# A ScalarE function set with logarithm and exponential together, loaded by hand at four places of a one-core diffusion layer

## The chip, the cores and the metric

The kernel runs on one core of one Trainium2 chip. The metric is the device time of one execution in microseconds (us), as a median over runs. Inside the core the trace has these engines: PE (TensorE matmul, with PEld for its weight loads), DVE (VectorE), ACT (ScalarE), POOL (GpSimd) and SP (SyncE, which issues most DMA transfers). Each engine takes its instructions in the order in which they were written to its queue; engines wait for each other through semaphores.

[...]

## The reference

One layer with 1024 latent tokens and 256 context tokens, width 1024. Cut to the parts in which a logarithm or an exponential stands:

```python
def rms_norm(x, w):
    y = xf * lax.rsqrt(jnp.mean(xf * xf, axis=-1, keepdims=True) + EPS)

px = modulate(rms_norm(x, norm1_w[i]), sh1, sc1) @ w_in[i]      # and the same for the context
dn_x, _, _ = gated_deltanet(px[..., :DN_IN], ...)               # conv + SiLU, decay exp(..), chunked scan
qx, kx, vx = na_qkv(px[..., DN_IN:], q_norm_w, k_norm_w)        # rms_norm per head of q and k
na_x = neighborhood_attention(qx, kx, vx, kc, vc, rpb, rows)    # softmax
x = x + g1 * (concat([dn_x, na_x]) @ w_out[i])
x = x + g2 * swiglu(modulate(rms_norm(x, norm2_w[i]), sh2, sc2), w_ffn_in[i], w_ffn_out[i])
...
```

## The kernel before

Everything is held with channels on the 128 partitions and tokens along the free dimension. Matmuls are in single precision, mostly as three products of a high and a low part, so each weight block is cut into `whi`/`wlo` (or `uhi`/`ulo`) by a CAST on ACT and a subtraction on DVE or POOL.

The program runs through these stages, in order of time:

- **Start.** Sums of squares, then the first norm: `rs` by a logarithm (L779) and an exponential (L781, times -0.5) on ACT, then the modulated tokens `hh`/`hl` (L752, L753, L759) and the first two blocks of the input projection.
- **Input projection.** A list of jobs: convolution blocks `k`, `q`, `v`, gates `z`, attention blocks `nk` and `nq`, and two wide jobs with tokens as rows. While PE multiplies job n, the job before it is finished. For `k`, `q`, `v` and `z` that takes the function SiLU (L529, L483). For `nk` and `nq` it is a norm by head: PE sums the squares `cr` into a PSUM bank `m` or `pr`, ACT takes the logarithm (L549) and then the exponential (L551 for `nq`, L553 for `nk`), DVE multiplies the block `cacc` by the result (L561), ACT rounds it to 16 bits (`hl`, L566 or L573), DVE forms the rest (L567, L574). Meanwhile two background generators run: the decay tables and block inverses (`decay_tables`, L836 to L888, exponentials; the inverse's copies `N`, L944, and its DVE chain L952/L954), and then `preps`, which build the triangular factors of each chunk: an exponential on `e` (L1022), `fx` copies (L1018), products in the PSUM banks `pr`, their copies `kk` on ACT (L1035) and `y` on DVE (L1043).
- **Scan and attention.** Two scans (forward and backward) run beside the neighbourhood attention; softmax is an exponential on ACT (L365), after a maximum on DVE (L363) and before a scaling on DVE (L367); PE then transposes (L106). The scan's copies on ACT are `u` (L1271) and `s` (L1283).
- **Output projection and second norm.** `normed(0)` and `normed(1)`: PE sums the squares `acc` (DVE, L1498), ACT takes logarithm and exponential (L1506, L1507) into `rs`, DVE scales the tokens `x` by it (L1614), ACT adds the shift and casts (L1618, L1619), DVE forms the low part (L1622).
- **FFN.** Products over saved sums of quadrants (L1638 forms a sum, L1608/L1609 cut it), SiLU (L1707, L1757), DVE additions out of PSUM (L1756, L1759), modulation work on weights `wad` that arrive by DMA (L253, L255), weights cut by L1464, L1468, L1469. From here to the end PE is fed from these streams.

The order on each queue is set by a scheduling layer that looks at the program with costs of its own; a few instructions are pinned to the written order by `tc.keep_in_program_order`. PSUM tiles are named by tag, with a number of buffers: in the input projection `blk` has 4, `m` and `pr` have 2 each. So a product into `pr` must wait until the product two before it was copied out.

Of the kernel before, what the change touches and what calls it, by code (L numbers as in the profile page):

```python
# [9 lines left out]
F32 = mybir.dt.float32  # L10
F32R = mybir.dt.float32r
F16 = mybir.dt.float16
I32 = mybir.dt.int32
AF = mybir.ActivationFunctionType
OP = mybir.AluOpType
# [76 lines left out]
def hybrid(ctx, tc, a, dbg):  # L92
    nc = tc.nc
    act, dve, pool, sp = nc.scalar, nc.vector, nc.gpsimd, nc.sync
# [12 lines left out]
            return tc.keep_in_program_order(i) if self.pinned else i  # L107

    pe = Tensor()

    def pools(stack, name, side=None, bufs=1, **kw):
        if side:
            kw["side"] = side
        return stack.enter_context(tc.tile_pool(name=name, bufs=bufs, reuse_waits="tile", **kw))
# [50 lines left out]
    nv_d = dram.tile([T, 512], F32, name="nv_d", tag="nv_d")  # L165
    nq_d = dram.tile([NAH, 2, ND, L], F16, name="nq_d", tag="nq_d")
    nk_d = dram.tile([2, NAH, ND, T], F16, name="nk_d", tag="nk_d")
    vw_d = dram.tile([4, 512, 512], F32, name="vw_d", tag="vw_d")
# [28 lines left out]
    def rsqrt(r, x, y):  # L197

        dve.tensor_scalar(y.bitcast(I32), x.bitcast(I32), 1, None, op0=OP.logical_shift_right)
        dve.tensor_scalar(r.bitcast(I32), y.bitcast(I32), -1.0, float(0x5F3759DF), op0=OP.mult, op1=OP.add)  # L200
        for _ in range(3):
# [97 lines left out]
    def attention(nw):  # L299

        def load(hd):
            qs = nw.tile([128, L], F16, name="qs", tag="qs", bufs=4)
            kh = nw.tile([128, T], F16, name="kh", tag="kh", bufs=4)
            kl = nw.tile([128, T], F16, name="kl", tag="kl", bufs=4)
            sp.dma_start(qs, nq_d[hd].rearrange("i d t -> (i d) t"))
            for i in range(2):
                sp.dma_start(kh[i * 64:i * 64 + 64], nk_d[0, hd])
                sp.dma_start(kl[i * 64:i * 64 + 64], nk_d[1, hd])
            return qs, kh, kl
# [111 lines left out]
    with ExitStack() as bs:  # L421
# [8 lines left out]
        def bank(name="m"):  # L430

            if len(psum) == 1:
                return psum[0].tile([128, 512], F32, name=name, tag="ps")
            return psum[1].tile([128, 512], F32, name=name, tag=name, bufs=4 if name == "blk" else 2)
# [19 lines left out]
        class Block:  # L454
# [22 lines left out]
            def evac(self):  # L477
                t0, kind, i = self.t0, self.kind, self.i
                if kind == "z":
                    zt = (zo[0].tile([128, T], F32, name="zt", tag="zt") if zo else  # L480
                          cp.tile([128, T], F32, name="zt", tag="kx", bufs=3))
                    for p, s0, n in self.pss:
                        act.activation(zt[:, s0:s0 + n], p[:, :n], AF.Silu)  # L483
                    sp.dma_start(zT_d[:, i], zt[:, t0:])
                    return
                self.acc = acc = cp.tile([128, T], F32, name="cacc", tag="cacc", bufs=2)
                conv = kind in "qkv"
                blk = {"q": 0, "k": 4, "v": 8}.get(kind, 0) + i
                if not conv or len(psum) == 1:
                    for p, s0, n in self.pss:  # L490
                        act.activation(acc[:, s0:s0 + n], p[:, :n], AF.Copy, scale=cw[:, blk, 2:3] if conv else 1.0)
                if not conv:
                    return
                if len(psum) == 1:
                    for p, s0, n in self.pss:
                        lo, hi = (0, CT) if s0 < CT else (CT, T)
                        for tap in (0, 1, 3, 4):
                            o = tap - 2
                            d0, d1 = max(lo, s0 - o), min(hi, s0 + n - o)
                            dve.scalar_tensor_tensor(acc[:, d0:d1], p[:, d0 + o - s0:d1 + o - s0],  # L500
                                                     cw[:, blk, tap:tap + 1], acc[:, d0:d1],
                                                     op0=OP.mult, op1=OP.add)
                    return
                raw = cp.tile([128, T], F32, name="cr", tag="cr", bufs=2)
                for p, s0, n in self.pss:
                    act.copy(raw[:, s0:s0 + n], p[:, :n])
                self.later = self.taps(raw, acc, blk)
# [18 lines left out]
            def silu(self):  # L526
                acc, t0 = self.acc, self.t0
                if self.kind in "qkv":
                    act.activation(acc[:, t0:], acc[:, t0:], AF.Silu)  # L529
                if self.kind in ("q", "nq", "nk"):  # L530
                    self.r = cp.tile([128, T], F32, name="cr", tag="cr", bufs=2)
                    act.activation(self.r[:, t0:], acc[:, t0:], AF.Square)

            def norm(self):

                kind, acc, t0, i = self.kind, self.acc, self.t0, self.i
                if kind in "vz":
                    return int
                if kind == "k":
                    sp.dma_start(kT_d[:, i], acc)  # L540
                    return int
                r = self.r
                if kind == "q":
                    sp.dma_start(qT_d[:, i], acc[:, t0:])
                    return int
                for s0, n in self.segs:
                    p = bank("pr" if kind == "nk" and s0 >= 768 else "m")
                    pe.matmul(p[:, :n], M[C_BD2], r[:, s0:s0 + n], start=True, stop=True)
                    act.activation(r[:, s0:s0 + n], p[:, :n], AF.Ln, bias=b_eps, scale=1.0 / ND)  # L549
                if kind == "nq":  # L550
                    act.activation(r[:, t0:], r[:, t0:], AF.Exp, scale=-0.5, bias=b_naq)  # L551
                else:
                    act.activation(r[:, t0:], r[:, t0:], AF.Exp, scale=-0.5)  # L553
                return self.split

            def split(self):
# [5 lines left out]
                                         op0=OP.mult, op1=OP.mult)  # L562
                hl16 = cp.tile([128, 2, T], F16, name="hl16", tag="kx", bufs=3)
                h16, l16 = hl16[:, 0], hl16[:, 1]
# [115 lines left out]
        with ExitStack() as xs:  # L680
# [52 lines left out]
            def sums(ps, k):  # L733

                for k in (k, k + 1):
                    sq = xp.tile([128, T], F32, name="sq", tag="sq", bufs=4)
                    act.activation(sq, xt[k], AF.Square)
                    if k % 2 == 0:
                        even = sq
                dve.tensor_tensor(sq, sq, even, OP.add)  # L740
                for p, (s0, n) in zip(ps, SEGS):
                    pe.matmul(p[:, :n], M[C_ONE], sq[:, s0:s0 + n], start=k == 1, stop=k == KT - 1)
# [32 lines left out]
            for k in (0, 2, 4, 6):  # L775
                sums(ps, k)
            first[0].prefetch(raws[0], lo_engine=dve)
            for p, (s0, n) in zip(ps, SEGS):
                act.activation(rs[:, s0:s0 + n], p[:, :n], AF.Ln, bias=b_eps, scale=1.0 / D)  # L779
            for x in (slice(0, CT), slice(CT, T)):  # L780
# [1103 lines left out]
```

## Time and profile before

| | |
|---|---|
| median of 3 runs | 1502.54 us (1499.14, 1502.54, 1506.05) |
| profiled execution | 1503.29 us, of which the span is 1501.5 us |
| mean granted TensorE clock | 0.994 |
| PE busy | 1452.1 us, 97% of the span |
| DVE busy | 1012.5 us, 67% |
| ACT busy | 696.9 us, 46% |
| table loads on ACT | 37 |

In the rows of a timeline the columns are: start in us from the span's beginning, duration, engine, source line, operation, what is written from what, shape, count, and in brackets the idle time of the engine just before with what ended it. Rows of equal neighbours are merged. A matmul in plain single precision gives two records. In a table of stretches (`A:B`) the columns are the length and then, for each engine, the busy us with the count of instructions; after them the granted clock of PE, the DMA engines' share and GB/s.

### The profile page before, as it was taken

The page shows a single profiled execution, that of the slowest core. Times are in us where ns is not written, and L with a number is a line of the kernel's source. Part 1 is how long each engine was busy: PE and PEld are TensorE (multiplying, and loading weights), DVE is VectorE, ACT ScalarE, POOL GpSimd, SP SyncE. Part 2 cuts the span into 40 slices and gives each one's busy share as a digit, 9 for nine tenths or more (in the row PEclk, how much of TensorE's full clock was granted, in tenths as well). Part 3 has the DMA queues.
Part 4 walks back from the last instruction along what each step waited for, and adds up shares of the span by engine and source line. Part 5 has one row for each costly group of instructions (what it writes and reads, how often), then busy time and mean ns, then how long its engine had stood idle before and what let it go on. Part 6 is the DMA issues. An engine that isn't in the chain of part 4 may idle for free.

```text
span 1501.5 us, 23098 instructions
## 1 busy us (share of the span) xinstructions
PE 1452.1 (97%) x8365; PEld 1201.8 (80%) x8365; DVE 1012.5 (67%) x1928; ACT 696.9 (46%) x1321; POOL 194.6 (13%) x223
## 2 busy tenths in 40 slices
PE   5999999989999999999999999999999999999998
PEld 2789788768877778888877787888888888888887
DVE  4887579465688437689965598656655557698652
ACT  6443362773366536567742473333333334354441
POOL 0154600343134221210100000000000000000000
PEclk9999999999999999999999999999999999999999
DMA  9377135455477789886349106333333334898742
GB/s 365 122 232 242 49 92 165 139 175 167 130 226 228 223 283 289 234 232 193 100 165 325 43 28 209 107 105 105 106 98 105 106 106 161 285 353 286 239 148 84
DMA packets 194019, 264.72 MB, mean 176 GB/s; under 512 B 15200, under 2 KB 104368, under 8 KB 192816
## 3 DMA queue, kind: packets, MB, share of 16 engines
q1 hardware_dynamic: 193056, 258.68, 53.6%
q10 hardware_dynamic: 848, 4.56, 0.9%
q8 instruction: 66, 1.08, 0.3%
q14 instruction: 49, 0.40, 0.1%
HBM read 199.70 MB, written 67.67 MB: 178 GB/s over the span
## 4 chain that ended last, share of the span: by engine, by line
PE 51%; DVE 6%; ACT 3%; DMA 2%; issue 1%; SPq 0%; ACTq 0%; DVEq 0%
PE ps L102 45%; PE sc L102 5%; PE sc L106 2%; DMA wad<-wa 1%; ACT pt L377 1%; ACT ex L365 1%; DVE ex L363 1%; DVE acc L255 1%; DVE x L1638 1%; DVE x L1614 0%; DVE ex L367 0%; DVE ulo L1469 0%; DVE lT L1609 0%; DMA zT_d<-zt 0%; DVE ws L1464 0%
## 5 line engine op out<-in xcount | busy, mean ns | idle before, releaser
L102 PE MATMUL ps<-hT,uhi 128*128 128x512 f32 x496 | 147.5, 391 | 2.1 <-DVE e L1759 2.1
L102 PE MATMUL ps<-lT,uhi 128*128 128x512 f32 x496 | 146.9, 390 | 0.0
L102 PE MATMUL ps<-hT,ulo 128*128 128x512 f32 x496 | 146.6, 390 | 0.0
L102 PE MATMUL blk<-hh,whi 128*128 128x512 f32 (+1 forms) x456 | 140.1, 397 | 2.4 <-ACT hh L753 1.7
L102 PE MATMUL blk<-hh,wlo 128*128 128x512 f32 (+1 forms) x456 | 129.4, 376 | 0.0
L102 PE MATMUL ps<-hB,uhi 128*128 128x512 f32 x436 | 129.1, 390 | 0.0
L102 PE MATMUL blk<-hl,whi 128*128 128x512 f32 (+1 forms) x456 | 129.0, 376 | 0.0
L102 PE MATMUL ps<-lB,uhi 128*128 128x512 f32 x436 | 128.9, 389 | 0.0
L102 PE MATMUL ps<-hB,ulo 128*128 128x512 f32 x436 | 128.7, 389 | 0.0
L1468 ACT CAST uhi<-ws 128x512 fp32r<-128x512 f32 x91 | 54.8, 623 | 145.5 <-PE ps L102 78.2
L1468 ACT CAST uhi<-wq 128x512 fp32r<-128x512 f32 x101 | 60.4, 621 | 132.4 <-PE ps L102 67.6
L1469 DVE TENSOR_TENSOR ulo<-wq,uhi 128x512 fp32r<-128x512 f32 x101 | 67.1, 687 | 66.1 <-ACT uhi L1468 36.6
L102 PEld LDWEIGHTS ps<-hT,uhi 128*128 128x128 f32 x496 | 93.3, 188 | 22.1 <-issue 2.9
L102 PEld LDWEIGHTS ps<-lT,uhi 128*128 128x128 f32 x496 | 93.4, 189 | 19.9 <-DVE lT L1622 0.5
L102 PEld LDWEIGHTS ps<-hT,ulo 128*128 128x128 f32 x496 | 93.4, 188 | 19.6
L102 PEld LDWEIGHTS ps<-hB,uhi 128*128 128x128 f32 x436 | 81.8, 188 | 17.4 <-issue 0.5
L102 PEld LDWEIGHTS ps<-lB,uhi 128*128 128x128 f32 x436 | 81.8, 188 | 17.3 <-DVE lB L1622 0.4
L102 PEld LDWEIGHTS ps<-hB,ulo 128*128 128x128 f32 x436 | 81.8, 188 | 17.0
L102 PEld LDWEIGHTS blk<-hh,wlo 128*128 128x128 f32 x456 | 80.2, 190 | 18.0 <-issue 1.7
L102 PEld LDWEIGHTS blk<-hl,whi 128*128 128x128 f32 x456 | 80.9, 190 | 16.1
L102 PEld LDWEIGHTS blk<-hh,whi 128*128 128x128 f32 x456 | 75.6, 190 | 19.5 <-ACT hh L753 3.7
L1469 DVE TENSOR_TENSOR ulo<-ws,uhi 128x512 fp32r<-128x512 f32 x91 | 60.8, 687 | 36.6 <-ACT uhi L1468 28.4
(343 smaller groups left out, 3034.9 us busy)
## 6 DMA issues: line engine op xcount, KB each, us to landing
wq<-w_fo SPq DMA_DIRECT2D x99, 256.0 KB, 4.8
wq<-w_gu SPq DMA_DIRECT2D x88, 256.0 KB, 3.0
wad<-wa SPq DMA_DIRECT2D x64, 256.0 KB, 4.8
t_d<-g SPq DMA_DIRECT2D x22, 512.0 KB, 3.6
fr<-t_d SPq DMA_DIRECT2D x44, 256.0 KB, 5.2
bt<-rpb SPq DMA_DIRECT2D x48, 192.0 KB, 4.2
f_d<-g SPq DMA_DIRECT2D x33, 256.0 KB, 2.1
fr<-f_d SPq DMA_DIRECT2D x33, 256.0 KB, 3.9
```

What stands on the lines that cost most here:

```text
L102: i = nc.tensor.matmul(*args, **kw)
L106: i = nc.tensor.transpose(*args, **kw)
L255: dve.scalar_tensor_tensor(acc2, x, sc, acc2, op0=OP.mult, op1=OP.add)
L363: dve.tensor_tensor_reduce(ex, sc, bt, 1.0, -3.0e38, OP.add, OP.max, m[:, 0:1])
L365: act.activation(ex, ex, AF.Exp, bias=m[:, 1:2], accum_out=m[:, 2:3])
L377: act.copy(pt, sc)
L1468: act.copy(hi, self.raw[key])
L1469: dve.tensor_tensor(lo, self.raw[key], hi.bitcast(F32), OP.subtract)
L1638: dve.tensor_tensor(B[at][:, k], B[x][:, k], B.get(y, B["B11"])[:, k], OP.subtract)
```

## The change

A function `ln_and_exp` puts an ACT_TABLE_LOAD of set 6, which holds logarithm and exponential both, into ACT's order, pinned there. It is called at four places: ahead of the first norm, after the SiLU of the last `k` block, ahead of the last `nq` norm, and after the SiLU of the last `z` block. The program builder sees the set that stands and adds a load of its own only where a function is missing from it.

```diff
+LN_EXP = 6
...
+    def ln_and_exp():
+        return tc.keep_in_program_order(act.add_instruction(mybir.InstLoadActFuncSet(
+            name=nc.get_next_instruction_name(), act_func_set_id=LN_EXP)))
...
                     for p, s0, n in self.pss:
                         act.activation(zt[:, s0:s0 + n], p[:, :n], AF.Silu)
+                    if i == 3:
+                        ln_and_exp()
                     sp.dma_start(zT_d[:, i], zt[:, t0:])
...
                 if self.kind in "qkv":
                     act.activation(acc[:, t0:], acc[:, t0:], AF.Silu)
+                    if self.i == 3 and self.kind == "k":
+                        ln_and_exp()
...
+                if kind == "nq" and i == 3:
+                    ln_and_exp()
                 for s0, n in self.segs:
                     p = bank("pr" if kind == "nk" and s0 >= 768 else "m")
...
             first[0].prefetch(raws[0], lo_engine=dve)
+            ln_and_exp()
             for p, (s0, n) in zip(ps, SEGS):
                 act.activation(rs[:, s0:s0 + n], p[:, :n], AF.Ln, bias=b_eps, scale=1.0 / D)
```

In the changed file the lines stand 5 to 12 further down (L549 is L560, L1506 is L1518). ACT's queue holds 17 table loads where it held 37. Gone are the second load of the first norm (L781), seven of eight in front of L549, all four in front of L553 and all four in front of L551, and the two pairs at L1506 and L1507: 20. Four stand elsewhere or under the helper's line: L779, L845 (now after the last `k` SiLU), the last L549, and L365 (now after the last `z` SiLU). The loads in front of SiLU (L529, L483, L1707) and of L1022 stay.

ACT in the norm of the first `nk` block, just ahead of the copies `N` of the block inverse, before:

```order
L491 ACTIVATE cacc<-blk 128x512 x2
L549 ACT_TABLE_LOAD
L549 ACTIVATE cr<-m,bias 128x256
L549 ACTIVATE cr<-m,bias 128x512
L549 ACTIVATE cr<-pr,bias 128x512
L532 ACTIVATE cr<-cacc 128x1280
L553 ACT_TABLE_LOAD
L553 ACTIVATE cr<-cr 128x1280
L566 CAST hl_1718<-cacc 128x1280
L944 COPY N<-m 80x128x4 x2
```

and after:

```order
L498 ACTIVATE cacc<-blk 128x512 x2
L560 ACTIVATE cr<-m,bias 128x256
L560 ACTIVATE cr<-m,bias 128x512
L560 ACTIVATE cr<-pr,bias 128x512
L541 ACTIVATE cr<-cacc 128x1280
L564 ACTIVATE cr<-cr 128x1280
L577 CAST hl_1720<-cacc 128x1280
L956 COPY N<-m 80x128x4 x2
```

Both loads are gone and nothing else moved.

ACT in the norm of the third `nq` block, with the copy `kk` out of a `pr` bank behind it, before:

```order
L219 CAST whi<-wraw 128x1024
L506 COPY cr<-blk 128x512 x2
L549 ACT_TABLE_LOAD
L549 ACTIVATE cr<-m,bias 128x512 x2
L1018 COPY fx_2517<-xt 32x4x32
L551 ACT_TABLE_LOAD
L551 ACTIVATE cr<-cr,bias 128x1024
L1035 COPY kk<-pr 128x4x96
L1018 COPY fx_2517<-xt 32x4x32 x3
L1022 ACTIVATE e<-e,GN 128x128 x4
L573 CAST hl_2827<-cacc 128x512 x2
L529 ACT_TABLE_LOAD
```

and after:

```order
L224 CAST whi<-wraw 128x1024
L513 COPY cr<-blk 128x512 x2
L560 ACTIVATE cr<-m,bias 128x512 x2
L1030 COPY fx_2519<-xt 32x4x32
L562 ACTIVATE cr<-cr,bias 128x1024
L1047 COPY kk<-pr 128x4x96
L1030 COPY fx_2519<-xt 32x4x32 x3
L1034 ACTIVATE e<-e,GN 128x128 x4
L584 CAST hl_2829<-cacc 128x512 x2
L536 ACT_TABLE_LOAD
```

Again the two loads are gone; the load for the SiLU that follows stays.

ACT from the last `z` block into the scan and the attention (`u` and `s` are the scan's copies, `ex` the softmax, `pt` and `na` the attention's copies), before:

```order
L483 ACTIVATE zt<-blk 128x512 x4
L1271 COPY u<-ps 128x512 x2
L365 ACT_TABLE_LOAD
L365 ACTIVATE ex,mx<-ex,mx 128x640 x2
L1283 COPY s_5036<-ps 128x512
L1283 COPY s_5046<-ps 128x512
L365 ACTIVATE ex,mx<-ex,mx 128x640 x2
L377 COPY pt<-sc 128x640 x2
L389 CAST na_5010<-sc 128x8x16
L377 COPY pt<-sc 128x640
L365 ACTIVATE ex,mx<-ex,mx 128x640 x2
L377 COPY pt<-sc 128x640
```

and after:

```order
L488 ACTIVATE zt<-blk 128x512 x4
L113 ACT_TABLE_LOAD
L1283 COPY u<-ps 128x512 x2
L370 ACTIVATE ex,mx<-ex,mx 128x640 x2
L1295 COPY s_5040<-ps 128x512
L1295 COPY s_5050<-ps 128x512
L370 ACTIVATE ex,mx<-ex,mx 128x640 x2
L382 COPY pt<-sc 128x640 x2
L394 CAST na_5014<-sc 128x8x16
L370 ACTIVATE ex,mx<-ex,mx 128x640
L382 COPY pt<-sc 128x640
L370 ACTIVATE ex,mx<-ex,mx 128x640
```

The load moved ahead of the two copies `u`. From the fifth softmax on, the scheduling layer puts exponentials and copies in a slightly different order, on PE, DVE and SP too; the stretch ends after some 14 of the 64 softmaxes, and behind it all queues agree again up to the removed loads. The only other differences are one matmul of the input projection that changes place with four, and two reciprocal steps of the decay tables (L860, L861) that come a little earlier on DVE.

## The prediction

> **What bounds the kernel now.** I read the page's head and the chain that ended last first, then the groups on ACT, then the timeline of each engine round every table load.
>
> ```profile
> span 1501.5 us, 23098 instructions
> PE 1452.1 (97%) x8365; PEld 1201.8 (80%) x8365; DVE 1012.5 (67%) x1928; ACT 696.9 (46%) x1321; POOL 194.6 (13%) x223
> PE 51%; DVE 6%; ACT 3%; DMA 2%; issue 1%; SPq 0%; ACTq 0%; DVEq 0%
> L549 ACT ACT_TABLE_LOAD x8 | 10.3, 1283 | 0.1
> L553 ACT ACT_TABLE_LOAD x4 | 5.1, 1283 | 0.1
> L551 ACT ACT_TABLE_LOAD x4 | 5.1, 1283 | 0.1
> ```
>
> PE is busy 97% of the span, and ACT is 3% of the chain. Every load takes 1283 ns, so 20 fewer free ACT of 25.7 us. That is no gain by itself: ACT idles more than half the time. A removed load is worth something only where PE stood still behind it, or where something that PE waits for later did. All idle time of PE is about 49 us (1501.5 less 1452.1), so I went through PE's waits one by one and asked which of them has a removed load ahead of it. Six do.
>
> **Start: worth 0.** The load of L781 goes (1.3 us).
>
> ```profile
> 27.44 1.36 ACT L781 ACTIVATE rs<-rs 128x256 f32<-128x256 f32 x2
> 29.79 1.81 DVE L752 SCALAR_TENSOR_TENSOR xt<-xt,w1s,rs 128x256 f32<-128x256 f32 x3
> ```
>
> `rs` is complete at 28.80, but DVE starts on it at 29.79, when the other operand `w1s` has come out of PE's modulation products. The cover is 1.0 us; what it hides only grows. Worth nothing from either side, and no loss, since ACT gets earlier.
>
> **Decay tables: 0.9 us, bounds 0 and 1.6.** The load of L845 leaves 144.6 and goes to 121.6, behind the last `k` SiLU, where ACT stands idle for 1.5 us before 124.5; that absorbs it, and PE shows no wait there.
>
> ```profile
> 146.04 0.84 ACT L617 COPY kk<-m 128x512 f32<-128x512 f32 x2
> 147.02 2.96 POOL L621 TENSOR_TENSOR kd<-kk,cst 128x1280 f32<-128x1280 f32 x1 [13.15 <-ACT nA L836]
> 146.94 0.85 PE L102 MATMUL blk<-hh,whi 128*128 128x256 f32 x3 [0.70 <-DVE gX L841]
> 156.84 0.41 PE L102 MATMUL m<-G,cst 128*128 128x40 f32 x2 [0.87 <-DVE G L859]
> ```
>
> The `kk` copies end at 146.88, just before PE's bank is free (146.94) and POOL's `kd` starts (147.02); the DVE chain behind it ends in `G`, for which PE waits 0.87. With the load gone the copies move up some 1.0 us, bounded by PE's products, and so does this chain. The upper end is both waits (0.70 + 0.87), the lower is none of them. I take 0.9, since the second wait contains what the first gives.
>
> **First `nk` norm: 1.8 us, bounds 1.0 and 1.84.**
>
> ```profile
> 182.32 1.28 ACT L549 ACT_TABLE_LOAD   x1
> 189.03 1.55 DVE L561 SCALAR_TENSOR_TENSOR cacc<-cacc,qkw,cr 128x1280 f32<-128x1280 f32 x1 [5.45 <-ACT cr L553]
> 190.62 1.26 ACT L566 CAST hl<-cacc 128x1280 f16<-128x1280 f32 x1 [1.62 <-DVE cacc L561]
> 191.78 1.06 ACT L944 COPY N<-m 80x512 f32<-80x512 f32 x2
> 192.41 1.15 PE L106 MATMUL m<-cst,WK 128*80 128x128 f32 x8 [1.84 <-ACT N L944]
> ```
>
> Two loads stand between 182.3 and the copies `N`: without them L561, the cast and the copies are 2.6 us earlier, the first `N` ends at 189.8, and PE, which arrives at 192.41 - 1.84 = 190.57, no longer waits. PE was late by 1.84, so the rest of the 2.6 is not gained. What is late next is the DVE chain of the inverse behind these copies. It starts from PE's own transposes and so moves with PE; if it did not, the 0.8 to 0.9 us between the two would be lost, hence 1.0.
>
> **Third `nq` norm: 2.6 us, bounds 0.9 and 5.1.**
>
> ```profile
> 319.27 1.28 ACT L551 ACT_TABLE_LOAD   x1
> 321.62 0.46 ACT L1035 COPY kk<-pr 128x384 f32<-128x384 f32 x1
> 322.13 1.06 PE L102 MATMUL pr<-y,kk 128*32 128x64 f32 x8 [4.03 <-ACT kk L1035]
> 318.45 2.85 DVE L520 SCALAR_TENSOR_TENSOR cacc<-cr,cw,cacc 128x1022 f32<-128x1022 f32 x2
> 326.04 0.55 DVE L1043 COPY y<-pr 32x384 f32<-32x384 f32 x1
> 328.35 0.44 PE L102 MATMUL pr<-y,kk 128*32 128x32 f32 x8
> 321.25:328.08 6.83, 5.95 (x20) 4.63 (x20) 5.83 (x8) 5.47 (x13) 0.00 (x0) 0.50 0.62 183
> ```
>
> This is the longest wait of PE. Two loads (316.4 and 319.3) hold up `kk`, and after it the granted clock is 0.50 for 6.83 us. Without them `kk` is done at 319.5 instead of 322.1, so PE's wait falls from 4.03 to about 1.5. But the next product into `pr` (328.35) also needs the other bank, which DVE frees with L1043. DVE cannot start L561 before its two L520 end (318.45 + 2.85 = 321.3), only 0.4 us earlier than it did; counting on through L561, L520, the two L574 and L1043 in their order, that bank is free at about 325.7 instead of 326.6. PE at full clock would be there at 323.0 and wait 2.7 us. It goes on at 325.8 instead of 328.35: 2.6 us. If this second wait again brings half clock for 3.41 us, half of that (1.7) is lost: 0.9. If DVE is not late after all, the full 2.6 of the loads and some 2.5 us that the slow clock cost come back: 5.1.
>
> **Entry to the scan: 1.3 us, bounds 0 and 1.9.**
>
> ```profile
> 543.07 0.59 ACT L1271 COPY u<-ps 128x512 f32<-128x512 f32 x1 [1.29 <-issue]
> 546.74 0.59 ACT L1271 COPY u<-ps 128x512 f32<-128x512 f32 x1 [3.08 <-DMA zT_d<-zt]
> 547.34 1.28 ACT L365 ACT_TABLE_LOAD   x1
> 550.49 0.74 PE L106 MATMUL sc<-cst,ex 128*128 128x128 f32 x5 [1.89 <-DVE ex L367]
> ```
>
> The load moves ahead of the `u` copies, into the 1.29 us that ACT idles before 543.07. There it just fits: queued behind it is the first `u`, and a delay of that copy by a few tenths reaches PE only at 546.1, so it is hidden. The first softmax starts at 547.3 instead of 548.6, and PE's wait falls from 1.89 to 0.6. Behind this the queues are reordered for about 50 us; PE is at 29.95 of 30 us there (below), so I count 0 for the order, and 0 to 1.9 in all.
>
> **Second norm: 1.1 us, and 3.8 us later on.**
>
> ```profile
> 850.72 2.74 DVE L1614 SCALAR_TENSOR_TENSOR x<-x,w2s,rs 128x512 f32<-128x512 f32 x4 [5.29 <-ACT rs L1507]
> 853.80 0.62 PE L102 MATMUL ps<-na,wlo 128*128 128x512 f32 x2
> 856.31 1.41 DVE L1517 SCALAR_TENSOR_TENSOR x<-ps,modp,x 128x512 f32<-128x512 f32 x2
> 860.93 1.10 PE L102 MATMUL ps<-acc,ones 128*128 128x512 f32 x2 [1.08 <-DVE acc L1498]
> 868.49 3.41 DVE L1614 SCALAR_TENSOR_TENSOR x<-x,w2s,rs 128x512 f32<-128x512 f32 x5 [2.76 <-ACT rs L1507]
> 934.59 1.28 DVE L1759 TENSOR_TENSOR e<-ps,e 128x512 f32<-128x512 f32 x2
> 935.42 0.57 PE L102 MATMUL ps<-hT,uhi 128*128 128x512 f32 x1 [2.08 <-DVE e L1759]
> 932.24:935.65 3.41, 1.33 (x6) 0.75 (x4) 3.34 (x6) 1.14 (x2) 0.00 (x0) 1.00 0.34 115
> 935.65:939.06 3.41, 3.38 (x8) 2.48 (x8) 3.41 (x7) 0.15 (x1) 0.00 (x0) 0.50 0.22 79
> 868.00:914.00 46.00, 45.97 (x203) 37.73 (x202) 45.41 (x75) 30.56 (x54) 0.00 (x0) 1.00 0.25 83
> ```
>
> The first pair of loads makes DVE begin L1614 at 850.72; without it, 2.6 us sooner. DVE's queue then reaches L1517, which needs PE's products of 853.80, done at 854.4: it starts at 854.5 instead of 856.31, 1.8 earlier. The chain to `acc` is 1.8 earlier with it, and PE's wait of 1.08 at 860.93 is gone.
>
> The second pair has no PE wait next to it, but DVE does: 2.76 idle at 868.49. ACT reaches that logarithm 1.8 us earlier and needs 2.6 less, so DVE starts about 4.4 us earlier, 3.3 ahead of a PE that gained 1.1. From there DVE is busy 45.4 of 46 us: a backlog that it carries until L1759, which frees the PSUM for which PE waits 2.08 at 935.42. That wait needs 2.08 of the 3.3. It is followed by 3.41 us at granted clock 0.50, worth 1.7 us of PE. Both gone: 3.8, bounds 0 (some wait of DVE on PE, ACT or a `wad` transfer eats the lead) and 3.8.
>
> The other removed loads (204 to 302, and L551 at 504.5) have no PE wait of over 0.5 us behind them: PE works on other products, and ACT is still ahead if that cover shrinks. Worth 0.
>
> **Sum.** 0.9 + 1.8 + 2.6 + 1.3 + 1.1 + 3.8 = 11.5 us. The profiled execution took 1503.29 us, 0.75 above the median of 1502.54: 1491.8 on its scale, 1491.0 on that of the median.
>
> **Rivals.**
>
> *The lead is lost before 935* (20%). DVE's lead of 3.3 us passes casts that wait for PE to free weight buffers and `wad` loads. Then the sum is 7.7 and the time 1494.8. For it: nothing of DVE's order changes. Against: DVE itself paces the issue of those transfers.
>
> *Only the plain terms hold* (13%). The `nq` norm runs into half clock (0.9) and the decay tables give nothing: 0.9 + 1.8 + 1.3 + 1.1 = 5.1, 1497.4.
>
> *The half clock does not hang on the 2.08 us wait* (8%). Then 1.7 less, 1492.7. The rows speak against it: the slow stretch starts in the slice in which PE was busy 1.33 of 3.41 us. [...]
>
> *More half clock goes* (6%): two further slow stretches (near 267 and 772) follow PE waits of 0.8 and 2.3 us, at 1.7 us each; with the 5.1 above in place of 2.6 the time falls to 1486 to 1488.
>
> *The change does not reach PE* (6%): all waits are taken over by other work, 1502.
>
> *Slower* (5%): the reordered stretch of the scan.
>
> ```profile
> 560.00:590.00 30.00, 29.95 (x304) 26.98 (x305) 22.19 (x67) 18.60 (x45) 4.17 (x4) 1.00 0.96 273
> POOL kt L1244 <- DMA kt<-k_d: 51.1, 6, 13.3
> ```
>
> The DMA engines are at 0.96 there, and POOL already waits up to 13.3 us for a `kt` load. SP's order changes in it; if two such loads came to stand in front of PE, that costs 26.6 less 11.5: 1518. Up to 11.5 us it only eats the gain, and below that the time is not above the old one. Against it: PE shows no such wait now.
>
> **How the numbers follow.** The forecast has 42%; its own range is 1487 to 1494. The range 1486 to 1500 takes in the lost lead, the plain terms and the larger gain, and leaves out the last two rivals. A measurement of this kernel tells about 0.5% (7.5 us, 1495.0) from no change. Faster: 40 of the forecast's 42, 7 of the next rival's 8 (1492.7), 9 of the lost lead's 20, and 6, is 0.62; slower 0.05; the rest 0.33.
>
> **What would show it.** 17 loads on ACT. PE's waits at 192, 860 and 935 gone; at 322 one of 1.5 and one of 2.7 us in place of 4.03; at 550 one of 0.6. DVE without idle time from 864 to 916. Wrong would be: a new PE wait above 1 us in 548 to 600, a wait at 935 that stays, or half clock where PE waited less than before.

## The result and the profile after

The changed kernel takes 1490.12 us (median of six runs, 1487.11 to 1492.81) beside 1503.76 us of the kernel before (six runs). The ratio is 0.9914, 95% interval 0.9892 to 0.9936: by the ratio 12.9 us faster, 9.6 to 16.2. In a second measurement it was 1489.38 us at a ratio of 0.9903 (0.9884 to 0.9923). The forecast was 1491.0 us, 11.5 us faster.

The head of the profile after, and the table loads left on ACT:

```profile
span 1486.4 us, 23079 instructions
PE 1446.1 (97%) x8365; PEld 1200.4 (81%) x8365; DVE 1015.1 (68%) x1928; ACT 670.2 (45%) x1301; POOL 195.2 (13%) x223
L536 ACT ACT_TABLE_LOAD x5 | 6.4, 1283 | 4.1 <-DVE cacc L507 4.1
L113 ACT ACT_TABLE_LOAD x4 | 5.1, 1283 | 0.1
L1034 ACT ACT_TABLE_LOAD x4 | 5.1, 1283 | 2.1 <-DMA e<-g_d 2.0
```

With one each at L199 and L1719 and two at L488 there are 17. ACT is 26.7 us less busy, and about half of that shows in the time. PE has the same 8365 instructions.

The profiled execution took 1488.22 us, so the two profiled runs lie 15.1 us apart, 1.4 more than the medians. To see where the 15.1 come from, take the same product of PE in both traces and subtract its start after from its start before: that is PE's lead. What the lead gains or loses at a place is what that place is worth in this pair of runs. Rows of PE and of what it waits for, in the timeline after, at the places of the prediction:

```profile
30.03 3.40 DVE L763 SCALAR_TENSOR_TENSOR xt<-xt,w1s,rs 128x256 f32<-128x256 f32 x5
157.85 0.41 PE L103 MATMUL m<-G,cst 128*128 128x40 f32 x2 [0.99 <-DVE G L871]
189.93 1.06 ACT L956 COPY N<-m 80x512 f32<-80x512 f32 x2
191.41 1.04 PE L107 MATMUL m<-cst,WK 128*80 128x128 f32 x8
314.66 0.46 ACT L1047 COPY kk<-pr 128x384 f32<-128x384 f32 x1
315.17 0.63 PE L103 MATMUL pr<-y,kk 128*32 128x64 f32 x8 [0.44 <-ACT kk L1047]
321.10 0.44 PE L103 MATMUL pr<-y,kk 128*32 128x32 f32 x8 [2.31 <-DVE y L1055]
541.60 0.74 PE L107 MATMUL sc<-cst,ex 128*128 128x128 f32 x5 [0.47 <-DVE ex L372]
568.40 0.32 PE L103 MATMUL sc<-pt,vc 128*64 128x128 f32 x1 [0.84 <-ACT pt L382]
839.80 2.74 DVE L1626 SCALAR_TENSOR_TENSOR x<-x,w2s,rs 128x512 f32<-128x512 f32 x4 [2.73 <-ACT rs L1519]
851.34 1.02 PE L103 MATMUL ps<-acc,ones 128*128 128x512 f32 x2
922.93 0.62 PE L103 MATMUL ps<-hT,uhi 128*128 128x512 f32 x2
```

A row without a bracket is one that PE reached without waiting: those at 191.41, 851.34 and 922.93 waited 1.84, 1.08 and 2.08 before. The subtraction, term by term:

| place (us before) | forecast | found |
|---|---|---|
| start, to 36 | 0 | -1.3 |
| decay tables, 147 and 157 | 0.9 | 0.4 |
| first `nk` norm, 192 | 1.8 | 2.0 |
| slow clock at 267 | not in the sum | 1.4 |
| `pr` product at 313 | not in the sum | 0.9 |
| third `nq` norm, 322 to 328 | 2.6 | 4.0 |
| entry to the scan, 550 | 1.3 | 1.6 |
| the scan behind it, to 772 | 0 | -0.5 |
| second norm, first half, 861 | 1.1 | 1.2 |
| `e` at 935, and the slow clock behind it | 3.8 | 2.2 + 1.9 |
| small ones: 0.6 between 862 and 877, 0.7 behind PE's last product | 0 | 1.3 |

Half clock has moved as well. Two rows of the stretches after, in slices of the same 3.41 us grid:

```profile
32.69:36.10 3.41, 3.41 (x10) 2.83 (x11) 3.41 (x5) 1.46 (x2) 0.00 (x0) 0.50 1.02 423
763.14:766.56 3.42, 2.84 (x7) 2.26 (x8) 1.91 (x3) 1.15 (x2) 0.00 (x0) 0.50 0.92 321
```

The granted clock (the 0.50 behind the engines) is low in these two, where before it was low near 267, 321 to 328, 772 and 936. The one at 32.69 is new, and costs about 1.0 of the 1.3 lost at the start. The rest, 0.3, was already there at 26 us, ahead of anything that waits for the first removed load. Nothing ties the slow slice to the change: the second run of this kernel, further down, does not have it, and the kernel without the first place, which has that load back, does.

### The profile page after: what moved, and what is told of

It reads as the page before. It is cut to its first block, busy times and chain, and to the rows that moved or that the text cites. A ratio compares the mean times of both kernels' runs of the same rounds, so it can differ in the third digit from the quotient of the medians.

```text
span 1486.4 us, 23079 instructions
## 1 busy us (share of the span) xinstructions
PE 1446.1 (97%) x8365; PEld 1200.4 (81%) x8365; DVE 1015.1 (68%) x1928; ACT 670.2 (45%) x1301; POOL 195.2 (13%) x223
## 3 DMA queue, kind: packets, MB, share of 16 engines
q8 instruction: 66, 1.08, 0.3%
## 4 chain that ended last, share of the span: by engine, by line
PE 57%; DVE 3%; ACT 2%; DMA 1%; issue 1%; SPq 0%; ACTq 0%; DVEq 0%
PE ps L103 51%; PE sc L103 5%; PE sc L107 2%; ACT pt L382 1%; ACT ex L370 1%; DVE ex L368 1%; DVE ex L372 0%; DMA wad<-wa 0%; DVE vn L1263 0%; DMA bt<-rpb 0%; DMA wraw<-w_out 0%; DMA y<-y_d 0%; PE ps L107 0%; DVE acc L260 0%; DVE x L1529 0%
```

## Experiments: one place at a time

**Without the place behind the last `z` SiLU.** The second norm and the first softmax load their own sets again.

```diff
-                    if i == 3:
-                        ln_and_exp()
                     sp.dma_start(zT_d[:, i], zt[:, t0:])
```

> Undoes the place behind the last z SiLU alone: the loads of the second norm (two pairs) and the one in the first softmax come back. If the terms of the prediction hold as the two traces show them (scan entry 1.6, first half of the second norm 1.2, DVE's lead at the last quadrant 2.4, and 1.7 more where half clock follows that wait), this is 5.2 to 6.9 us slower than the changed kernel: 1495.3 to 1497.0, PE waits again about 1.9 at the first softmax, 1.1 at acc and 2 at e. Rival, that the lead gained by DVE has nothing to do with the 2.08 us wait at e (a wad transfer sets it): the wait at e stays away and it is 2.8 us slower, 1492.9.

Measured: 1495.31 us, ratio to before 0.9949 (0.9933 to 0.9964), 5.2 us above the changed kernel: the lower end. Three of its waits:

```profile
542.72 0.52 PE L107 MATMUL sc<-cst,ex 128*128 128x128 f32 x3 [1.89 <-DVE ex L372]
863.13 3.41 DVE L1624 SCALAR_TENSOR_TENSOR x<-x,w2s,rs 128x512 f32<-128x512 f32 x5 [2.76 <-ACT rs L1517]
929.17 1.06 PE L103 MATMUL ps<-hT,uhi 128*128 128x512 f32 x2 [1.13 <-DVE e L1769]
```

DVE's idle time of 2.76 in front of the second half of the norm is back to the hundredth, and with it a wait of PE for `e`, 66 us later. In every kernel with the `z` place this wait is absent, so the lead of DVE is what removes it. The wait is 1.13 and not 2.08, though DVE has the same instructions in the same order as before: in between it stood 2.11 us for a `wad` transfer here,

```profile
912.75 0.75 DVE L260 SCALAR_TENSOR_TENSOR acc<-wad,sc,acc 128x512 f32<-128x512 f32 x1 [2.11 <-DMA wad<-wa]
918.94 0.75 DVE L255 SCALAR_TENSOR_TENSOR acc<-wad,sc,acc 128x512 f32<-128x512 f32 x1 [3.13 <-DMA wad<-wa]
```

where it stood 3.13 before (second row). So both accounts hold in part: the loads decide whether the wait is there, the transfer moves it by 1 us (1.13 here, 2.08 before). No half clock followed the 1.13.

**Without the place behind the last `k` SiLU.**

```diff
-                    if self.i == 3 and self.kind == "k":
-                        ln_and_exp()
```

> Undoes the place behind the last k SiLU alone: the loads of the decay tables and of the first nk and nq norms come back up to the third nq norm. By the two traces 0.6 (decay tables) + 1.9 (PE's wait for N) = 2.5 us slower than the changed kernel, 1492.6, and the wait of 1.84 for N is back. Rival, that this gain is taken up again before the third nq norm (PE then waits longer at kk): 0 slower, 1490.1, with a longer wait behind it. If the slow clock near 267 in the trace of before belongs to these loads too, 1.4 to 1.7 more, 1494.2.

Measured: 1498.0 us, ratio 0.996 (0.9943 to 0.9976), 7.9 above the changed kernel. More than all three expected:

```profile
193.07 1.15 PE L107 MATMUL m<-cst,WK 128*80 128x128 f32 x8 [1.84 <-ACT N L954]
321.50 1.05 PE L103 MATMUL pr<-y,kk 128*32 128x64 f32 x8 [3.99 <-ACT kk L1045]
```

The wait for `N` is back, as expected, but so is the one for `kk`, which I had put down to the place ahead of the last `nq` norm. In the changed kernel ACT has a load at 122.88, behind the last `k` SiLU, and the next at 319.25, for a SiLU; here 15 loads of 1283 ns stand ahead of that one. So the one load serves all norms up to the third `nq` norm.

The lead of the changed kernel over this one grows by 6.3 us between 40 and 330 us, with a slice of half clock behind `kk` in it. Behind that, this profiled run has a PE wait of 1.37 at 475 for a copy `fx`, which the second run of the changed kernel has too, and longer waits for `whi` and `x` (4.18 and 2.79 for 2.66 and 1.49). So not all of the 7.9 need belong to this place.

**Without the place ahead of the last `nq` norm.**

```diff
-                if kind == "nq" and i == 3:
-                    ln_and_exp()
```

> Undoes the place ahead of the last nq norm alone: the Ln and Exp there load their own sets again. The traces give 4.0 us here (the prediction said 2.6): about 4.0 slower than the changed kernel, 1494.1, with a PE wait of about 4 at kk and half clock behind it. Rival, that place k alone already holds the set up to here (so that only what follows a SiLU between them reloads): under 1 us slower, 1490 to 1491.

Measured: 1488.65 us, ratio 0.9906 (0.9876 to 0.9936), as the changed kernel. My main expectation fell and the rival held. This place replaces a pair of loads at about 494 us by one, where PE waits for nothing. It does change the order of the scan, 60 us later (see the entry to the scan below).

**Without the first place.**

```diff
             first[0].prefetch(raws[0], lo_engine=dve)
-            ln_and_exp()
```

> Undoes the first place alone: one load more (1.28 us) between the logarithm and the exponential of the first norm. The prediction said this is worth 0, since DVE waits there for w1s, with 1.0 us of cover: 0 to 0.3 us slower, 1490.1 to 1490.4. Rival, the load lies on the path in full: 1.3 us slower, 1491.4, and rs, not w1s, is what DVE waits for last.

Measured: 1490.74 us, ratio 0.9925 (0.9901 to 0.9949). One load stands between logarithm and exponential:

```profile
26.72 1.28 ACT L792 ACT_TABLE_LOAD   x1
28.01 1.36 ACT L792 ACTIVATE rs<-rs 128x256 f32<-128x256 f32 x2
30.20 3.40 DVE L763 SCALAR_TENSOR_TENSOR xt<-xt,w1s,rs 128x256 f32<-128x256 f32 x5
31.28 0.39 PE L103 MATMUL blk<-hh,whi 128*128 128x256 f32 x1 [0.62 <-ACT hh L764]
```

`rs` is done at 29.37 and DVE begins at 30.20, 0.8 us later: the cover is there, and PE waits 0.62 for `hh` with the load and without it. Worth 0, as forecast.

**Only the two places that count.** The last two edits together; the trace has 19 loads on ACT (the expectation says 20).

> Keeps only the places behind the last k SiLU and behind the last z SiLU; 20 loads on ACT. If those two carry all of the gain: as the changed kernel, 1490.1, between 1489 and 1491.5. Rival, that the four places work together (the first and the nq place give room that the others use): 2 us or more slower, 1492 and above.

Measured: 1489.49 us, ratio 0.9897 (0.9868 to 0.9927). Two places do what four do, within intervals of some 4 us each way. In the trace the waits for `N`, `acc` and `e` are gone, and the one for `kk` is 0.32.

**The `k` place moved to the third `nq` norm.** All earlier norms load their own sets again.

```diff
-                    if self.i == 3 and self.kind == "k":
-                        ln_and_exp()
...
-                if kind == "nq" and i == 3:
+                if kind == "nq" and i >= 2:
                     ln_and_exp()
```

> The place behind the last k SiLU goes to the third nq norm: the loads of the decay tables, of the four nk norms and of two nq norms come back, the pair ahead of kk at the third nq norm stays away. If the terms are independent: the wait of 1.84 for N is back, decay tables 0.6, N 1.9, and 0.9 at the pr product near 313 are lost, 3.4 slower than the changed kernel, 1493.5; PE's wait at kk is as short as in the changed kernel (under 0.7) and the second one, for y, is 2.3 to 2.7. Rival, that kk is late because of the whole row of earlier loads: PE waits about 4 at kk again, 7.7 slower as without the place, 1498.

Measured: 1495.54 us, ratio 0.994 (0.9921 to 0.9959), between the two expectations.

```profile
194.21 1.04 PE L107 MATMUL m<-cst,WK 128*80 128x128 f32 x7 [1.83 <-ACT N L954]
320.91 0.63 PE L103 MATMUL pr<-y,kk 128*32 128x64 f32 x8 [1.25 <-ACT kk L1045]
326.01 0.44 PE L103 MATMUL pr<-y,kk 128*32 128x32 f32 x8 [1.52 <-DVE y L1053]
```

The wait for `N` is back in full. Those for `kk` and `y` together are 2.77, about as in the changed kernel (0.44 + 2.31), but split otherwise. With the earlier loads ACT comes to the norm later, and `kk` is later. `y` is not later, because the scheduling layer has changed DVE's order here: three steps L527 stand ahead of L570 (L561 before), where it was two, and `y` comes right behind L570, where it came after the two L574.

```profile
320.01 4.17 DVE L527 SCALAR_TENSOR_TENSOR cacc<-cr,cw,cacc 128x1022 f32<-128x1022 f32 x3
```

So the wait for `kk`, 1.25 here and 3.99 without the place, shows the pair of loads ahead of it as a term of its own. Its worth in time is not shown cleanly, since DVE's order moved with it. How the 7.9 us of this place divide into before and at the third `nq` norm isn't settled to better than 2 or 3 us: the intervals of the two kernels overlap.

## Experiments: half clock, and a faster version

**The first `w_out` loads ahead of the first `w_gu` loads.** In the changed kernel PE waits 2.66 us for `whi` at the start of the output projection. SP stands 20.9 us at the first `wq` load, which waits for PE, and the `wraw` loads are queued behind it. The edit gives `load_w` an argument `fix`; here it pins these loads and their casts to the written order, and the first eight `w_gu` loads are pinned too, behind them.

```diff
-                sp.dma_start(r, src)
-            act.copy(h, r)
+                fix(sp.dma_start(r, src))
+            fix(act.copy(h, r))
...
-        ws = [load_w(a["w_out"][b, :, :4], kt=4, lo_engine=dve) for b in range(2)]
+        ws = [load_w(a["w_out"][b, :, :4], kt=4, lo_engine=dve, fix=tc.keep_in_program_order) for b in range(2)]
...
-                sp.dma_start(t, a["w_fo"][f[1], i, h] if isinstance(f, tuple) else a["w_gu"][f, i, h])
+                d = sp.dma_start(t, a["w_fo"][f[1], i, h] if isinstance(f, tuple) else a["w_gu"][f, i, h])
+                if n == 8:
+                    tc.keep_in_program_order(d)
```

> The changed kernel with the first two w_out loads and their casts held ahead of the first w_gu loads, on SP and on ACT. If PE's wait for whi at the start of the output projection (2.66 in the changed kernel) and the half clock behind it come from standing behind those two loads and two casts: the wait falls to 0.7 to 1.3, no half clock follows, 3 us faster than the changed kernel, 1487 (1486 to 1488.5). Rival, that a transfer's own time sets it: the wait stays at 2.2 or more, 1490.

Measured: 1487.79 us, ratio 0.9888 (0.9862 to 0.9914). SP's queue in the changed kernel (first two rows) and in this one (third), and PE here:

```profile
758.34 0.84 SPq L1452 DMA_DIRECT2D wq<-w_gu  x2
759.28 0.93 SPq L223 DMA_DIRECT2D wraw<-w_out  x2
```

```profile
744.88 2.08 SPq L223 DMA_DIRECT2D wraw<-w_out  x2
762.56 0.73 PE L103 MATMUL sc<-gah,whi 128*128 128x512 f32 x2 [0.30 <-ACT whi L224]
```

The transfers start 14 us earlier and the wait falls to 0.30, below what I expected. No half clock follows. The median is where I expected it, 2.3 us below that of the changed kernel and 1.7 below that of the two places on the same chip, but the intervals don't separate them.

**Both together, beside the changed kernel on one chip.** The two places that count, with the loads above.

> The two places that count (behind the last k SiLU, behind the last z SiLU), with the first two w_out loads and casts ahead of the first w_gu loads. If the two effects add: 2 to 3 us faster than the changed kernel on the same chip (one pt wait of 0.84 in the first softmaxes less, and 2.0 to 3.3 at whi). Rival, that the gain at whi is given back at the next wait (the one for x, 1.5 in the changed kernel): within 1 us of it.

Measured: 1485.35 us (1483.36 to 1489.13), ratio 0.9879 (0.9859 to 0.9898).

> The changed kernel once more, beside the one above on one chip. The waits of PE come back at the same places and lengths within some tenths, those on transfers within 1 us. If half clock follows where PE stood idle 1.9 us or more within one slice of the 3.41 us grid, it comes behind the wait for whi or for y in this run only where the wait lies so in the grid, and the places may differ from the first trace. Rival, that it is the length of the wait: the same places as before, behind whi alone.

Measured: 1489.38 us, ratio 0.9903 (0.9884 to 0.9923). The version above is 4.0 us faster by the medians, the fastest kernel here, though the intervals still overlap. That is more than the 2 to 3 expected. PE's next wait, for `x`, is 2.76 in it:

```profile
783.37 0.70 PE L103 MATMUL ps<-gah,whi 128*128 128x512 f32 x2 [2.76 <-DVE x L1528]
```

It is 1.49 and 2.19 in the two runs of the changed kernel. But it is 2.4 in the kernel with the two places alone, and 1.5 in the one with the `w_out` loads alone, so whether some of the gain at `whi` is given back there, as the rival has it, is not shown. In its profiled run no half clock falls behind either wait, which is part of that run's lead. In this second run of the changed kernel its waits came back: 3.1 at `whi` for 2.66, 2.52 at `y` for 2.31, 2.2 at `x` for 1.5. One came that the first trace lacks, 1.37 at a `pr` product at 468.94.

The two runs of the one kernel differ in half clock. Slice by slice round the wait for `y`, first in the first run, then in this one:

```profile
319.41:322.82 3.41, 1.73 (x14) 1.47 (x15) 3.35 (x6) 1.68 (x2) 0.00 (x0) 1.00 0.73 163
322.82:326.24 3.42, 3.42 (x21) 2.53 (x20) 1.33 (x3) 1.57 (x2) 1.14 (x4) 1.00 0.62 237
```

```profile
316.85:320.26 3.41, 0.98 (x11) 0.86 (x12) 3.38 (x5) 1.86 (x3) 0.00 (x0) 1.00 0.62 159
320.26:323.67 3.41, 3.41 (x10) 2.64 (x9) 1.47 (x4) 2.11 (x2) 1.11 (x4) 0.50 0.83 281
```

In the first run the grid cut the wait in two, and PE was busy 1.73 of the slice: the next slice has the full clock. In the second it lay in one slice, PE was busy 0.98, and the next slice has 0.50. The same wait in all the kernels that have it alone:

| run | wait for `y` | most idle time in one slice | half clock behind it |
|---|---|---|---|
| without `z` | 2.19 | 2.19 | yes |
| changed, first run | 2.31 | 1.68 | no |
| two places | 2.34 | 1.89 | yes |
| without first | 2.35 | 1.33 | no |
| without `nq` | 2.39 | 1.45 | no |
| changed, second run | 2.52 | 2.44 | yes |
| `w_out` first | 2.53 | 2.14 | yes |
| two places and `w_out` first | 2.64 | 1.61 | no |

The length does not sort them: 2.19 brings half clock and 2.64 does not. The idle time within one slice does. Over all eleven traces, from 40 to 1470 us, worked out from PE's records: 17 slices at full clock had 1.85 us or more idle (the least 1.89), and half clock followed all 17. About 70 had 1.0 to 1.85 (the most 1.82), and it followed 2, both with 1.14, at the `N` products near 265.

Ahead of 40 us this border fails. In seven of the eleven traces half clock follows a slice near 28 to 30 us in which PE stood idle only 0.9 to 1.3 us; in two others it does not follow 1.07 and 1.21. So idle time within a slice accounts for the long waits of this kernel and is not the whole rule. What else counts stays open.

## Why the prediction was right, and where it was off

The way to it held. The six places named as having a PE wait behind a removed load gave 0.4, 2.0, 4.0, 1.6, 1.2 and 4.1 in the first two profiled runs, 13.3 for a forecast of 11.5, and the first norm gave nothing by its loads. The two large groups come out of the runs: 7.9 us without the `k` place, of which the trace shows 6.3 up to the third `nq` norm (forecast 0.9 + 1.8 + 2.6 = 5.3), and 5.2 without the `z` place (1.3 + 1.1 + 3.8 = 6.2). That the sum came so near has some luck in it: the 1.4 gained at 267, the 1.3 lost at the start and the 0.5 lost in the scan were not in it, and nearly cancel.

- **Start.** Right as to the load: the run without the first place shows 0.8 us of cover. What the start lost (1.3) is in no step of the change.
- **Decay tables, 0.9.** Half of it: PE's first wait fell from 0.70 to 0.35, the second, for `G`, stayed (0.87, now 0.99). "The second wait contains what the first gives" was wrong; PE, earlier by the first, waits longer at the second.
- **First `nk` norm, 1.8.** Right; the wait of 1.84 is gone, and comes back at 1.84 and 1.83 in the two kernels with the loads.
- **Third `nq` norm, 2.6.** Too small, 4.0. The step that failed is "DVE cannot start L561 before its two L520 end": I took their end, 321.3, as fixed. In the trace of before they stand behind L515, which waits for a copy `cr` of ACT, and ACT comes to that copy earlier when the loads of the norms ahead of it are gone too.

```profile
315.31 1.05 ACT L506 COPY cr<-blk 128x512 f32<-128x512 f32 x2
316.39 2.03 DVE L515 TENSOR_SCALAR cacc<-cr,cw 128x1024 f32<-128x1024 f32 x1 [2.09 <-ACT cr L506]
309.06 1.05 ACT L513 COPY cr<-blk 128x512 f32<-128x512 f32 x2
310.14 2.03 DVE L522 TENSOR_SCALAR cacc<-cr,cw 128x1024 f32<-128x1024 f32 x1 [1.67 <-ACT cr L513]
312.20 2.85 DVE L527 SCALAR_TENSOR_TENSOR cacc<-cr,cw,cacc 128x1022 f32<-128x1022 f32 x2
310.47 1.04 ACT L513 COPY cr<-blk 128x512 f32<-128x512 f32 x2
310.64 2.39 POOL L226 TENSOR_TENSOR wlo<-wraw,whi 128x1024 fp32r<-128x1024 f32 x1 [5.39 <-ACT whi L224]
310.89 2.30 DVE L1026 TENSOR_TENSOR xt<-xt,NB 128x128 f32<-128x128 f32 x1
313.11 1.12 DVE L522 TENSOR_SCALAR cacc<-cr,cw 128x1024 f32<-128x1024 f32 x1
314.26 2.60 DVE L527 SCALAR_TENSOR_TENSOR cacc<-cr,cw,cacc 128x1022 f32<-128x1022 f32 x2
```

  (Two rows of before, three of the second run of the changed kernel, five of its first run.) The second run shows it plainly. At the `pr` product near 313 PE is 5.0 us ahead there. On the scale of before, `cr` starts at 314.0, DVE waits for it as before, and the two L520 (L527 now) end at 320.0: all 1.3 earlier. With the `k` place moved to this norm, so that only the earlier loads are back, `cr` is again at 315.3 on that scale (316.86, where PE is 1.55 behind).

  In the first run (PE 3.3 ahead) the gain takes another way. `cr` starts at 313.8 on the scale of before, 1.6 earlier, but DVE does not wait for it: it stood 2.0 us for a transfer of `xc` and then took 2.30 for an `xt` step that takes 0.29 before, beside POOL's `wlo`. So L522 starts at 316.4, no earlier than before. It then takes 1.12 where it took 2.03 beside `wlo`, and the two L520 end at 320.1, 1.2 earlier. `kk` too was 3.7 earlier and not 2.6 (done at 318.4). The wait for `y` is 2.31 (2.7 forecast), and no half clock followed it in this run; in others it did, which is the lower bound's case.

- **Entry to the scan, 1.3.** The wait fell from 1.89 to 0.47. But "I count 0 for the order" was wrong by 0.5 in this pair of runs: the reordered stretch has one more wait for `pt`, 0.84 at 568.40. All six traces with the new order have it. The four other kernels (without `z`, and the three without the last `nq` place), whose order there stays close to the old one, lack it. Why the `nq` place changes that order is not shown. PE's lead over the kernel before grows to 9.8 us at 560 and is 8.4 at 772.
- **First half of the second norm, 1.1.** Right, 1.2.
- **`e` at 935, 3.8.** The wait is gone in every kernel that has the `z` place, by DVE's lead. Of its own 2.08, about 1 us depends on a transfer (1.13 in the kernel without that place). The slow clock behind it, 1.9 in this pair of runs for a forecast of 1.7, follows a slice that holds the whole 2.08.
- **Half clock.** The rival that it "does not hang on the 2.08 us wait" is answered: from 40 us on, half clock followed all 17 slices at full clock with 1.89 us or more idle, and the slice ahead of 935.65 has 2.08. Whether the gain at 267, part of the rival at 6%, comes from the loads is open: PE's wait there is 0.80 before and 0.77 after, with 1.14 and 1.11 idle in the slice, and half clock followed in two of the three traces with the loads ahead of it and in none of the other eight. That rival is also added up wrongly: 11.5 with 5.1 for 2.6 and twice 1.7 gives 1485.1, not 1486 to 1488. In the traces of before and after the slow stretches last 3.41 us, once 6.83, and start on one grid in each: at 266.64, 321.25, 771.81 and 935.65 before, which are 16, 132 and 48 slices of 3.413 us apart, and at 32.69 and 763.14 after, 214 slices apart. The shortest wait for `y` with half clock behind it is 2.19.
- **The first line to fail** in "what would show it" was DVE without idle time from 864 to 916: it stands 3.3 us there for `wad` transfers. PE did not wait for it.

What stays open: about 1.5 us of the 5.2 of the `z` place. Between the traces of the changed kernel and of the one without that place, PE's lead grows by 1.2 at the first half and by 2.4 from there to behind `e`. The 1.5 of the entry is given back by 700 us, by the wait for `pt` and smaller ones. That makes 3.7, and the waits for `whi` and `x`, which differ by up to 0.7 each between the two runs of the changed kernel, hide the rest.

## What to carry to other kernels

Here ACT became 26.7 us less busy and the kernel 12.9 us faster: removed work on an engine with idle time is worth what PE waited behind it. So walk PE's waits and ask at each what stands ahead of the producer; then check one step further up, whether the same edit also moves the inputs that you hold fixed. Watch the order too: a pinned instruction may make the scheduling layer move others; here PE got one more wait for `pt` by it, 0.84. Find the shortest list of places: here two of four, 1489.49 us beside 1490.12. Look at what stands behind the head of a queue: SP stood 20.9 us at a `wq` load, and the two `wraw` loads behind it started 14 us earlier when they were put ahead of it.

## What the hardware showed beyond that

In these traces a table load costs its 1283 ns and no gap: in the run without the first place, where the input of the activation behind the load is ready, that activation begins 0.01 us after the load's end (26.72 + 1.28 against 28.01).

Two DVE instructions in the rows at the third `nq` norm took longer beside POOL's `wlo` (2.39 us, at 310.64 after and 315.48 before): L1026 2.30 after, where the same step took 0.29 before, at 314.01; L515 2.03 before, where the same step (L522) took 1.12 after, once `wlo` had ended, and 0.75 at 382.86, where POOL did nothing.

Half clock behind the wait for `y` came in one of the two runs of the changed kernel: not where 1.68 us of idle time lay in one slice of the 3.41 us grid (a wait of 2.31), and in the other where 2.44 did (2.52). Over 48 runs of the kernel before, each 0.001 of mean granted clock goes with 1.2 us (a line through all, correlation -0.91; clocks of 0.989 to 0.998, some 10 us). The wait of 2.08 at `e`, once removed, gave 2.2 us of PE's lead in the first two traces, and the half clock that had followed it 1.9 more; half of a slice is 1.7.
